# Convolution of a gated feed-forward layer: the accumulator of the three taps in PSUM instead of SBUF

## Chip, core and metric

The kernel runs on one core of a Trainium2 chip. The metric is the device time of one execution in microseconds (us); the median of three runs of the kernel before is 1090.98 us (1090.66 to 1093.48). A profile is one further execution, recorded by the hardware profiler: the one shown here took 1091.43 us, and the span of its recorded work is 1089.6 us.

The engines are named as the profile names them: PE multiplies matrices and writes its products to PSUM, PEld is the loading of its weights, DVE is the vector engine, ACT the scalar engine, POOL the GpSimd engine, and SP's queue issues the DMA transfers.

## What is computed

One layer of a diffusion backbone works on 512 latent tokens and 128 prompt tokens with the same weights, everything in 32-bit floats. Attention and a pooling mixer come first; the change is in the feed-forward part that follows. For a token matrix h (640 x 1024) it is

```
a, up = split(h @ w_ffn_in)                      # 1024 -> 2816 and 2816
a  = a[t-1] * w[0] + a[t] * w[1] + a[t+1] * w[2] + b     # along the tokens, per channel
x  = x + gate2 * ((silu(a) * up) @ w_ffn_out)
```

The convolution `dwconv3` runs over the 512 latent tokens and over the 128 prompt tokens as two separate sequences, with zeros beyond their ends. A final RMSNorm follows.

## The kernel before

**Tiles.** The 2816 channels are 22 tiles of 128 channels, which lie on the 128 partitions; the 640 tokens lie along the free dimension. Every 32-bit matrix product is made of three products of rounded halves (the high part of the weight with the high and the low part of h, and its low part with the high part of h). The 22 tiles form three groups of 8, 7 and 7 (`GROUPS`); after each group `out2_steps` multiplies the finished tiles with their rows of `w_ffn_out` and adds the result to x.

**One tile.** The two token halves (320 each) of `a` and `up` are not made by eight block products but by seven (a Strassen-like scheme). `product(i, p)` (line 1068) is one of the seven, p = 1 to 7, each 12 matmuls of 128x320, in two PSUM banks of tile i, `PS[i][0]` (named pf`i`A) and `PS[i][1]` (pf`i`C), and a bank of its own for product 2 (pb, from `bank1`, line 108, a pool of two banks). Both pf banks come from a pool of six (`banks`, line 997). The steps that read the products are `copy1`, `copy5`, `copy6` (ACT, PSUM to SBUF) and `add2`, `add3`, `add7` (DVE, one operand in PSUM). They leave the 640 values of `a` in the SBUF tile `av`, and part of `up` in the SBUF tile `c`. Product 3 ends in pf`i`C and `add3` is the last to read it there. Product 7 ends in pf`i`A, `add7` reads it, and only then may product 4 add to the same bank.

**The weights** need work too: POOL builds sums of weight blocks (`sums`, line 1030, four additions of 128x512 for a tile, both inputs in SBUF), ACT rounds them (`hi`, 1041), DVE subtracts to get the low parts (`lo`, 1058; tiles wlo_f and ul). The raw weights come by DMA into a pool of three buffers.

**The convolution** of tile i is `conv(i)` (line 1117): ACT writes `av * w[1] + b` into the SBUF tile `cv` (one instruction, 128x640), then four DVE instructions SCALAR_TENSOR_TENSOR add the taps in place: for the latent tokens 511 values shifted by one each way, for the prompt tokens 127 each way. Each reads `av` and `cv` and writes `cv`. `silu(i)` (1126) is one ACT instruction over `cv` in place; `glu2` (1129) and `glu1` (1132) multiply the halves of `cv` with `up`; `ghi` and `glo` (1136, 1139) split the product for the second matrix multiplication.

**Order.** All these steps run in a written order: `Pin` (142) makes every engine keep the order in which the code calls it, so that in the profile they all stand under line 150, and groups are told apart by their tiles. `cycle(i, ...)` (1425) is the order of one tile: it makes products 1, 2, 5, 6 and 3 of tile i and products 7 and 4 of tile j = i - 1, and in between the convolution of tile j and the weights of tile n = i + 1. On DVE the order of a cycle is: `add3(j)`, the four taps of tile j, `add2(i)`, `add7(j)`, `lo(n, 1)`, `glu2(j)`, `lo(n, 2)`, `lo(n, 3)`, then `glu1(j)`, which waits for product 4 of tile j, and `lo(n, 4)`. On PE it is products 1 and 2 of i, 7 of j, 5, 6 and 3 of i, 4 of j. Tiles 0 and 1 (`DIRECT`) are made directly and stand in another written order, `start` (1482); tile 2 is the first of the cycles' kind.

Of the kernel before, what the change touches and what calls it, by code (L numbers as in the profile page):

```python
# [13 lines left out]
AF = mybir.ActivationFunctionType  # L14
ALU = mybir.AluOpType
# [6 lines left out]
LAT = 512  # L22
PRO = 128
TOK = LAT + PRO
# [12 lines left out]
V_C, V_CC, V_N1, V_N2, V_PS, V_CW, V_CB, V_SUB, V_END = 0, 8, 16, 24, 32, 36, 102, 124, 125  # L37
# [30 lines left out]
def trunk_kernel(ctx: ExitStack, tc: tile.TileContext, a: dict, o: list):  # L68
# [39 lines left out]
    def bank1(name):  # L108
        return psB.tile([P, 512], F32, tag="B", name=name)
# [43 lines left out]
    dve, act, pool = Pin(nc.vector), Pin(nc.scalar), Pin(nc.gpsimd)  # L153
# [45 lines left out]
    vcol = const.tile([P, V_END], F32, tag="vcol", name="vcol")  # L199
# [820 lines left out]
    DIRECT = 2  # L1020
    R, S, W2, PS, PB, PD, AV, C22, CVS, GT = {}, {}, {}, {}, {}, {}, {}, {}, {}, {}
# [93 lines left out]
        dve.tensor_tensor(AV[i][:, HALF:], AV[i][:, HALF:], PS[i][1][:, :HALF], ALU.add)  # L1115

    def conv(i):
        av = AV.pop(i)
        cv = CVS[i] = pools["ffn"].tile([P, TOK], F32, tag="cv", name=f"cv{i}", bufs=3)
        w = [vcol[:, V_CW + j * NF + i:V_CW + j * NF + i + 1] for j in range(3)]  # L1120
        act.activation(cv, av, AF.Identity, bias=vcol[:, V_CB + i:V_CB + i + 1], scale=w[1])
        for s0, s1 in ((0, LAT), (LAT, TOK)):
            dve.scalar_tensor_tensor(cv[:, s0 + 1:s1], av[:, s0:s1 - 1], w[0], cv[:, s0 + 1:s1], ALU.mult, ALU.add)
            dve.scalar_tensor_tensor(cv[:, s0:s1 - 1], av[:, s0 + 1:s1], w[2], cv[:, s0:s1 - 1], ALU.mult, ALU.add)

    def silu(i):
        act.activation(CVS[i], CVS[i], AF.Silu)

    def glu2(i):
        dve.tensor_tensor(CVS[i][:, HALF:], CVS[i][:, HALF:], C22.pop(i), ALU.mult)  # L1130
# [294 lines left out]
    def cycle(i, first, end, after):  # L1425
# [17 lines left out]
        elif j is not None and j > first and first != DIRECT:  # L1443
            glo(j - 1)
        do(j, conv)
        do(n, sums, 0)
        add2(i)
# [5 lines left out]
        do(n, hi, 1)  # L1453
        do(n, lo, 1)
        do(j, silu)
        do(j, glu2)
        do(n, hi, 2)
# [24 lines left out]
    def start():  # L1482

        sums(2, 0)
        load(3, 0)
        conv(0)
        product(0, "G", "H")
        hilo(2, 2)
        sums(2, 1)
        load(3, 1)  # L1490
        product(1, "E", "F")
        copy6(1)
        silu(0)
        hi(2, 3)
        glu_direct(0)
# [10 lines left out]
        product(2, 5)  # L1506
        copy5(2)
        conv(1)
        hi(3, 2)
        lo(2, 4)  # L1510
        lo(3, 2)
        silu(1)
        sums(3, 1)
        product(2, 6)
# [68 lines left out]
```

## Time and profile before

| | |
|---|---|
| median of three runs | 1090.98 us (1090.66 to 1093.48) |
| profiled execution | 1091.43 us, span 1089.6 us |
| PE busy | 1038.0 us, 95% of the span |
| DVE busy | 851.6 us, 78% |
| ACT busy | 543.5 us, 50% |
| POOL busy | 320.8 us, 29% |
| the cycles of the three groups | 654 to 743, 806 to 894, 945 to 1031 us |
| PE / DVE busy there | 82.2 / 79.3 of 89 us, 85.1 / 81.1 of 88 us, 83.4 / 81.2 of 86 us |

The feed-forward part takes the last 450 us of the span. In the three stretches of cycles both PE and DVE are busy nearly all the time. An engine's busy time is the time that its instructions take in the record, and that includes the time in which an instruction has begun but is held up. Where an engine stands idle before an instruction, the profile names the instruction that released it.

### The profile page before, as it was taken

Reading aid. Unit: us, or ns where it says so; the run is one execution under the profiler, and the core shown is the slowest. Engines: PE = TensorE matmul, PEld = TensorE weight load, DVE = VectorE, ACT = ScalarE, POOL = GpSimd, SP = SyncE. Lnnn points to the kernel's source line nnn. Section 1 sums busy time; section 2 is a strip of 40 time slices with the busy share of each in tenths; the row PEclk is TensorE's granted clock in tenths of the full one; section 3 lists DMA queues with packets and bytes.
Section 4 is the critical chain, followed back from the end, with each engine's and each line's share of the span. In section 5 each row is a group of like instructions: output and inputs, shape, how many; then the busy total and the mean of one; then the engine's idle time right before and its main releaser. Section 6 shows DMA issues by size and latency. Waiting matters only on the chain.

```text
span 1089.6 us, 16713 instructions
## 1 busy us (share of the span) xinstructions
PE 1038.0 (95%) x6559; PEld 967.0 (89%) x6559; DVE 851.6 (78%) x1193; ACT 543.5 (50%) x906; POOL 320.8 (29%) x256
## 2 busy tenths in 40 slices
PE   6979999999999999999999999899989999999997
PEld 4778899999999999999998899898779998899986
DVE  5978978988887577776773579998889984699947
ACT  8646666666765552222242465554345542255524
POOL 4544224323222630000000005443374420444202
PEclk9999999999999999999999999999999999999999
DMA  9831212202112135545554022223442322323312
GB/s 312 247 88 51 62 32 69 59 25 71 38 43 59 41 96 157 165 140 159 154 190 141 1 78 59 83 92 93 127 128 82 94 68 68 97 78 94 119 38 97
DMA packets 128481, 106.10 MB, mean 97 GB/s; under 512 B 4174, under 2 KB 110206, under 8 KB 128403
## 3 DMA queue, kind: packets, MB, share of 16 engines
q1 hardware_dynamic: 126450, 101.93, 30.8%
q0 software_dynamic: 1232, 1.80, 0.8%
q8 instruction: 51, 0.84, 0.3%
q10 hardware_dynamic: 720, 1.31, 0.3%
q14 instruction: 28, 0.22, 0.1%
HBM read 101.36 MB, written 3.67 MB: 96 GB/s over the span
## 4 chain that ended last, share of the span: by engine, by line
PE 54%; DVE 28%; ACT 8%; issue 7%; POOL 1%; DMA 1%; SPq 0%; ACTq 0%; DVEq 0%; POOLq 0%
PE ps_g L157 10%; DVE cv L150 7%; PE psyb L157 5%; PE psk L157 3%; PE psu L157 3%; PE psya L157 3%; DVE wlo_f L150 3%; PE s L157 2%; PE acc L157 2%; PE po L157 2%; DVE nm L688 2%; PE psv L157 2%; PE psq L157 2%; ACT cv L150 1%; PE pat L160 1%
## 5 line engine op out<-in xcount | busy, mean ns | idle before, releaser
L150 POOL TENSOR_TENSOR s<-raw_fu 128x512 f32<-128x512 f32 x20 | 33.3, 1666 | 309.1 <-DVE spare L150 155.7
L150 DVE SCALAR_TENSOR_TENSOR cv<-av,vcol,cv 128x511 f32<-128x511 f32 (+1 forms) x80 | 88.8, 1130 | 12.1 <-ACT cv L150 10.8
L157 PE MATMUL ps_g<-hT,whi_g 128*128 128x320 f32 x512 | 96.7, 311 | 0.0
L157 PEld LDWEIGHTS ps_g<-hT,whi_g 128*128 128x128 f32 x512 | 80.2, 188 | 2.0 <-issue 1.5
L690 ACT ACTIVATE p<-s,nm 128x640 f32<-128x640 f32 (+1 forms) x80 | 56.7, 709 | 40.0 <-DVE nm L688 39.4
L688 DVE TENSOR_REDUCE nm<-s 128x1 f32<-128x640 f32 (+1 forms) x80 | 56.5, 709 | 12.4 <-PE s L157 11.0
L157 PE MATMUL psv<-whi_v,hT 128*128 128x256 f32 x320 | 66.0, 286 | 0.0
L157 PE MATMUL ps_g<-hT,wlo_g 128*128 128x320 f32 x256 | 58.3, 309 | 0.0
L150 DVE TENSOR_TENSOR wlo_f<-s,whi_f 128x1024 fp32r<-128x1024 f32 x40 | 51.0, 1298 | 4.7 <-ACT whi_f L150 4.6
L157 PE MATMUL s<-ks,qd 128*128 128x320 f32 x144 | 44.2, 318 | 10.7 <-DVE ks L599 7.1
L157 PEld LDWEIGHTS psv<-whi_v,hT 128*128 128x128 f32 x320 | 53.2, 192 | 0.3 <-ACT whi_v L126 0.3
L157 PE MATMUL psyb<-on,whi_pb 128*128 128x320 f32 x256 | 48.0, 309 | 0.0
L150 ACT CAST whi_f<-s 128x1024 fp32r<-128x1024 f32 x40 | 41.8, 1044 | 12.0 <-POOL s L150 11.9
L157 PE MATMUL psv<-wlo_v,hT 128*128 128x256 f32 x160 | 45.5, 284 | 0.9 <-DVE wlo_v L127 0.9
L157 PE MATMUL s<-ks,ql 128*128 128x320 f32 x144 | 42.9, 308 | 0.0
L157 PEld LDWEIGHTS ps_g<-hT,wlo_g 128*128 128x128 f32 x256 | 42.8, 188 | 0.0
L157 PE MATMUL psk<-hT,whi_k 128*128 128x320 f32 x224 | 42.6, 312 | 0.0
L157 PEld LDWEIGHTS psyb<-on,whi_pb 128*128 128x128 f32 x256 | 40.3, 188 | 0.5
L697 ACT ACTIVATE p<-p,z 128x640 f32<-128x640 f32 (+1 forms) x40 | 29.7, 744 | 20.0 <-DVE z L696 19.8
L157 PEld LDWEIGHTS s<-ks,qd 128*128 128x128 f32 x144 | 27.6, 192 | 13.4 <-POOL ry_q L562 6.8
L698 DVE SCALAR_TENSOR_TENSOR p<-p,z,p 128x640 f32<-128x640 f32 (+1 forms) x40 | 35.0, 878 | 5.4 <-ACT p L697 5.1
L150 POOL TENSOR_TENSOR acc_g<-acc_g,part_g 128x512 f32<-128x512 f32 x16 | 27.9, 1743 | 37.7 <-ACT part_g L150 36.8
(985 smaller groups left out, 3409.9 us busy)
## 6 DMA issues: line engine op xcount, KB each, us to landing
raw_fa<-in_w_ffn_in_dram SPq DMA_DIRECT2D x22, 512.0 KB, 3.8
raw_fu<-in_w_ffn_in_dram SPq DMA_DIRECT2D x22, 512.0 KB, 3.8
raw_fo<-in_w_ffn_out_dram SPq DMA_DIRECT2D x20, 512.0 KB, 3.6
raw_g<-in_w_in_dram SPq DMA_DIRECT2D x16, 512.0 KB, 4.9
raw_g<-in_w_ada_dram SPq DMA_DIRECT2D x16, 512.0 KB, 3.7
araw_sh<-in_w_ada_dram SPq DMA_DIRECT2D x8, 512.0 KB, 7.6
araw_sc<-in_w_ada_dram SPq DMA_DIRECT2D x8, 512.0 KB, 8.3
raw_v<-in_w_in_dram SPq DMA_DIRECT2D x8, 512.0 KB, 6.3
```

Of the source, the lines that this page charges most:

```text
L150: pin(getattr(self.eng, op)(*args, **kw))
L157: pin(nc.tensor.matmul(out, s, m, start=start, stop=stop, skip_group_check=more))
L160: pin(nc.tensor.transpose(out, x, ident))
L688: nc.vector.tensor_reduce(nm[:, i:i + 1], s, AX.XY, ALU.max, negate=True)
L690: nc.scalar.activation(p.rearrange("p (b n) -> p b n", b=s.shape[1]), s, AF.Exp, bias=nm[:, i:i + 1], accum_out=z[:, i:i + 1])
L697: nc.scalar.activation(p, p, AF.Copy, scale=z[:, 1:2])
L698: nc.vector.scalar_tensor_tensor(A[h, t], A[h, t], z[:, 0:1], p, ALU.mult, ALU.add)
```

## The change

For tiles 2 to 21 the running sum of the convolution is kept in PSUM: the 512 latent tokens in the bank pf`i`C, which `add3` was the last to read, and the 128 prompt tokens in a further bank `cvp` from the pool of two that product 2 uses. ACT's first step becomes two instructions (128x512 and 128x128), one for each bank. The four DVE instructions read `av` in SBUF and the sum in PSUM and write the sum in PSUM. `silu` becomes two instructions that read PSUM and write the SBUF tile `cv`, as the later steps expect it. Tiles 0 and 1 are unchanged.

```diff
     def conv(i):
         av = AV.pop(i)
         cv = CVS[i] = pools["ffn"].tile([P, TOK], F32, tag="cv", name=f"cv{i}", bufs=3)
         w = [vcol[:, V_CW + j * NF + i:V_CW + j * NF + i + 1] for j in range(3)]
-        act.activation(cv, av, AF.Identity, bias=vcol[:, V_CB + i:V_CB + i + 1], scale=w[1])
-        for s0, s1 in ((0, LAT), (LAT, TOK)):
-            dve.scalar_tensor_tensor(cv[:, s0 + 1:s1], av[:, s0:s1 - 1], w[0], cv[:, s0 + 1:s1], ALU.mult, ALU.add)
-            dve.scalar_tensor_tensor(cv[:, s0:s1 - 1], av[:, s0 + 1:s1], w[2], cv[:, s0:s1 - 1], ALU.mult, ALU.add)
+        if i < DIRECT:
+            SUMS[i] = cv[:, :LAT], cv[:, LAT:]
+        else:
+            SUMS[i] = PS[i][1], bank1(f"cvp{i}")[:, :PRO]
+        segs = tuple(zip(SUMS[i], (av[:, :LAT], av[:, LAT:])))
+        for c, x in segs if i >= DIRECT else ((cv, av),):
+            act.activation(c, x, AF.Identity, bias=vcol[:, V_CB + i:V_CB + i + 1], scale=w[1])
+        for c, x in segs:
+            dve.scalar_tensor_tensor(c[:, 1:], x[:, :-1], w[0], c[:, 1:], ALU.mult, ALU.add)
+            dve.scalar_tensor_tensor(c[:, :-1], x[:, 1:], w[2], c[:, :-1], ALU.mult, ALU.add)
+
+    SUMS = {}
 
     def silu(i):
-        act.activation(CVS[i], CVS[i], AF.Silu)
+        lat, pro = SUMS.pop(i)
+        cv = CVS[i]
+        for c, x in ((cv[:, :LAT], lat), (cv[:, LAT:], pro)) if i >= DIRECT else ((cv, cv),):
+            act.activation(c, x, AF.Silu)
```

On ACT, around the convolution of tile 16 (in the cycle of tile 17), the rows before are these; vcol holds the taps and the bias, whi_f and s belong to the weights of tile 18:

```order
L150 COPY av_9667<-pf17A 128x320
L150 ACTIVATE cv_9670<-av_9536,vcol 128x640
L150 COPY c_17_9693<-pf17C 128x320
L150 CAST whi_f_18_9695<-raw_fa_9588 128x1024
L150 ACTIVATE cv_9670<-cv_9670 128x640
L150 CAST whi_f_18_9701<-s_18_9676 128x1024
```

and in the changed kernel, at the same place:

```order
L150 COPY av_9709<-pf17A 128x320
L150 ACTIVATE pf16C<-av_9575,vcol 128x512
L150 ACTIVATE cvp_9713<-av_9575,vcol 128x128
L150 COPY c_17_9737<-pf17C 128x320
L150 CAST whi_f_18_9739<-raw_fa_9630 128x1024
L150 ACTIVATE cv_9712<-pf16C 128x512
L150 ACTIVATE cv_9712<-cvp_9713 128x128
L150 CAST whi_f_18_9746<-s_18_9720 128x1024
```

Each of the two ACT steps of the tile has become two instructions at its old place; nothing else on ACT moved.

On DVE the rows of the same cycle are, before (pb is product 2 of tile 17, pf16A holds product 7 of tile 16):

```order
L150 TENSOR_TENSOR av_9536<-av_9536,pf16C 128x320
L150 TENSOR_TENSOR g_9396<-cv_9538,g_9395 128x640
L150 SCALAR_TENSOR_TENSOR cv_9670<-av_9536,vcol,cv_9670 128x511 x2
L150 SCALAR_TENSOR_TENSOR cv_9670<-av_9536,vcol,cv_9670 128x127 x2
L150 TENSOR_TENSOR av_9667<-av_9667,pb_9641 128x320
L150 TENSOR_TENSOR c_16_9561<-c_16_9561,pf16A 128x320
L150 TENSOR_TENSOR wlo_f_18_9696<-raw_fa_9588,whi_f_18_9695 128x1024
L150 TENSOR_TENSOR cv_9670<-cv_9670,c_16_9561 128x320
```

and in the changed kernel:

```order
L150 TENSOR_TENSOR av_9575<-av_9575,pf16C 128x320
L150 TENSOR_TENSOR g_9435<-cv_9577,g_9434 128x640
L150 SCALAR_TENSOR_TENSOR pf16C<-av_9575,vcol,pf16C 128x511 x2
L150 SCALAR_TENSOR_TENSOR cvp_9713<-av_9575,vcol,cvp_9713 128x127 x2
L150 TENSOR_TENSOR av_9709<-av_9709,pb_9683 128x320
L150 TENSOR_TENSOR c_16_9602<-c_16_9602,pf16A 128x320
L150 TENSOR_TENSOR wlo_f_18_9740<-raw_fa_9630,whi_f_18_9739 128x1024
L150 TENSOR_TENSOR cv_9712<-cv_9712,c_16_9602 128x320
```

DVE's instructions keep number, shape and order; the four taps have another place for their sum. On PE, POOL and SP the order is the same in both kernels. PE has one wait more: product 2 of tile 4 lies in the bank that `cvp` of tile 2 had, and waits for the ACT instruction that reads it. From then on `cvp` and product 2 keep to one bank each of the two.

## Rows read from the trace of the kernel before

**Rows 1.** The page's part 4: the chain that ended last, by engine.
```profile
PE 54%; DVE 28%; ACT 8%; issue 7%; POOL 1%; DMA 1%; SPq 0%; ACTq 0%; DVEq 0%; POOLq 0%
```

**Rows 2.** Two cycles: stretch, its length, busy us (instructions) by engine, granted clock, DMA.
```profile
846.00:858.27 12.27, 12.27 (x87) 12.27 (x85) 11.94 (x15) 6.39 (x10) 5.85 (x4) 1.00 0.29 85
980.29:993.05 12.76, 12.48 (x86) 12.22 (x85) 12.43 (x15) 6.72 (x11) 6.39 (x4) 1.00 0.29 83
```

**Rows 3.** Weight loading's waits, 684 to 1035: total us, times, longest.
```profile
PEld pf2A L157 <- DVE c L150: 3.2, 1, 3.2
...
PEld pf8A L157 <- DVE c L150: 2.0, 1, 2.0
PEld pf15A L157 <- DVE c L150: 1.7, 1, 1.7
PEld pf3A L157 <- DVE c L150: 1.5, 1, 1.5
...
PEld pf19A L157 <- DVE c L150: 0.8, 1, 0.8
PEld pf4A L157 <- DVE c L150: 0.8, 1, 0.8
...
PEld pf5A L157 <- DVE c L150: 0.6, 1, 0.6
PEld pf17A L157 <- DVE c L150: 0.5, 1, 0.5
PEld pf16A L157 <- DVE c L150: 0.5, 1, 0.5
PEld pf12A L157 <- DVE c L150: 0.4, 1, 0.4
PEld pf18A L157 <- DVE c L150: 0.2, 1, 0.2
```

**Rows 4.** DVE's timeline, 680 to 690 us: start, duration, instruction, [idle before <- releaser].
```profile
681.67 5.07 DVE L150 SCALAR_TENSOR_TENSOR cv<-av,vcol,cv 128x511 f32<-128x511 f32 x4 [0.64 <-ACT cv L150]
...
687.06 0.47 DVE L150 TENSOR_TENSOR c<-c,pf2A 128x320 f32<-128x320 f32 x1
...
689.28 1.21 DVE L150 TENSOR_TENSOR wlo_f<-s,whi_f 128x1024 fp32r<-128x1024 f32 x1
```

**Rows 5.** PE's timeline, 684 to 690 us, the last matmul before the wait.
```profile
684.34 0.31 PE L157 MATMUL pf3C<-mg,wlo_f 128*128 128x320 f32 x1
```

**Rows 6.** DVE's timeline, 964 to 990 us: the taps of tile 16.
```profile
971.82 5.77 DVE L150 SCALAR_TENSOR_TENSOR cv<-av,vcol,cv 128x511 f32<-128x511 f32 x4 [0.26 <-ACT cv L150]
```

**Rows 7.** POOL's timeline, 938 to 995 us: one of four additions beside them.
```profile
972.80 1.63 POOL L150 TENSOR_TENSOR s<-s,raw_fa 128x512 f32<-128x512 f32 x1
```

**Rows 8.** DVE's timeline, 878 to 900 us: the taps of tile 13, POOL idle.
```profile
885.73 2.18 DVE L150 SCALAR_TENSOR_TENSOR cv<-av,vcol,cv 128x511 f32<-128x511 f32 x4 [0.26 <-ACT cv L150]
```

**Rows 9.** DVE's timeline, 373 to 403 us: the same operation with pr, pm in PSUM.
```profile
382.48 1.01 DVE L899 SCALAR_TENSOR_TENSOR on<-oraw,sub,pr 128x320 f32<-128x320 f32 x2 [1.51 <-PE pr L157]
...
386.34 1.01 DVE L921 SCALAR_TENSOR_TENSOR mix<-pm,vcol,mix 128x320 fp32r<-128x320 f32 x2 [0.48 <-ACT mix L920]
```

**Rows 10.** POOL's timeline, 373 to 403 us: what ran beside the second of them.
```profile
385.96 1.58 POOL L902 TENSOR_TENSOR on<-on,on 128x640 fp32r<-128x640 f32 x1 [3.88 <-PE pm L157]
```

**Rows 11.** Instructions on tile cv: duration ns min/median/max, first and last start, forms.
```profile
L150 DVE SCALAR_TENSOR_TENSOR cv<-av,vcol,cv x80: 340/1273/1684, 681.7 to 1035.5; 128x511 f32<-128x511 f32 x40, 128x127 f32<-128x127 f32 x40
L150 ACT ACTIVATE cv<-cv x22: 737/738/744, 663.3 to 1035.9; 128x640 f32<-128x640 f32 x22
...
L150 ACT ACTIVATE cv<-av,vcol x20: 919/924/926, 680.7 to 1032.2; 128x640 f32<-128x640 f32 x20
```

**Rows 12.** Instructions of line 433, ACT with scale and bias, columns as above.
```profile
L433 ACT ACTIVATE hT<-xT,sh,sc x16: 477/642/818, 24.1 to 55.4; 128x512 fp32r<-128x512 f32 x8, 128x128 fp32r<-128x128 f32 x8
```

**Rows 13.** The stretch 829.36 to 832.77 us, columns as in Rows 2.
```profile
829.36:832.77 3.41, 3.41 (x15) 3.41 (x14) 3.41 (x6) 2.03 (x4) 0.00 (x0) 0.50 0.51 149
```

**Rows 14.** DVE's timeline, 796 to 846 us: a low part of weights while POOL adds.
```profile
811.44 2.32 DVE L150 TENSOR_TENSOR wlo_f<-s,whi_f 128x1024 fp32r<-128x1024 f32 x1
```

## Prediction, made before the changed kernel ran

> **What bounds the kernel now.** I read the chain of waits first: PE holds 54% of it and DVE 28% [rows 1], so the question is where DVE holds PE up. The windows by cycle answer it for the feed-forward part. A cycle has 84 matmuls. Where PE never waits, it takes 12.27 us, 0.146 us a matmul; elsewhere it takes 12.76 us and DVE is busy for 12.43 of them [rows 2]. So the cycles run at the pace of DVE, and PE's own pace lies 0.49 us lower. The waits of the weight loads name the place: eleven times PE stands before product 4 of a tile (pf2A to pf19A) until DVE has done `add7` (c) [rows 3]. In DVE's order the four taps of the convolution stand just ahead of `add2` and `add7`, so their length is what PE waits for.
>
> The timeline of DVE shows why they are long. Beside POOL's four additions the four taps of tile 16 take 5.77 us; with POOL idle those of tile 13 take 2.18 us [rows 6 to 8]. One tap takes from 0.34 us (127 values, alone) to 1.68 us [rows 11]; from the 2.18 us a 511-wide one alone is 2.18 / 2 - 0.34 = 0.75 us. Both inputs of each tap are in SBUF, and so are those of POOL's additions.
>
> **The taps with their sum in PSUM.** The trace has the same operation with one input in PSUM: two of 320 values take 1.01 us with POOL idle and 1.01 us while POOL runs a 1.58 us subtraction with both inputs in SBUF [rows 9, 10]. So one input in PSUM takes POOL's hold off DVE. I price a tile's four taps at 2.18 us, against 5.77: 3.6 us less on DVE for each of the 14 or so tiles whose convolution meets POOL's additions; the last two of each group do not (tile 13 is one).
>
> What the trace does not show is a DVE instruction that writes PSUM, or reads and writes one bank. Its ends: below, rows 9 give 1.01 us for two of 320, and nothing there makes PSUM dearer, so 2.18 us or some tenths under it; above, 5.77 us, the length under POOL. I take 2.18, the value of the row that is nearest in operation.
>
> [...] A straight line from 0.34 us at 127 values to 0.75 at 511 gives 0.55 at 320, 1.09 for two, and the row with PSUM has 1.01 [rows 8, 9, 11]: no surcharge is seen. [...]
>
> **ACT.** One instruction of 0.92 us becomes one of 512 values and one of 128; with scale and bias such rows lie between 0.48 and 0.82 us [rows 11, 12], so 1.30 us at most in sum, 0.38 more. DVE needs only the first to start, 0.82 us, so it starts 0.1 us earlier. SiLU goes from 0.74 us to two instructions; from PSUM I have no row of it, and bound it by 0.74 for each piece, so 0.74 us more at the most; with the two fixed parts I take 0.1 to 0.2. ACT is busy for 6.7 of 12.76 us in a cycle [rows 2], and with 0.4 to 1.1 us more it still has 4.5 us free: nothing on the path. Without that cover it would be 20 x 0.5 = 10 us.
>
> **Banks.** pf`i`C is next written by product 5 of a tile three cycles later, so holding it until `silu` costs nothing. Product 2 of tile 4 now waits for the SiLU of tile 2. That follows the taps and is due by 683.75 + 1.5 = 685.3 (times as worked out below); the product starts two products, 24 matmuls, behind PE's restart, at 684.6 + 3.5 = 688.1. After that `cvp` and product 2 use different banks. 0 us, and if the cover went, one wait once.
>
> **The sum.** The eleven waits: 3.2 + 2.0 + 1.7 + 1.5 + 0.8 + 0.8 + 0.6 + 0.5 + 0.5 + 0.4 + 0.2 = 12.2 us [rows 3]. What is late next decides how much of it comes back.
>
> - First wait (tile 2): the taps start 0.1 us earlier than 681.67, at 681.57, and end at 683.75. `add7` ended 0.79 us behind the taps (687.53 against 686.74) [rows 4], so now at 684.54. PE itself is ready 0.146 us after its last matmul began, at 684.49 [rows 5]. Left: 0.05 us and the way of the signal, 0.1 us of 3.2.
> - The other ten: the taps give 3.6 us back, each wait is 2.0 us or less. Nothing is left.
> - Then PE sets the pace: DVE's cycle is 12.76 - 0.26 (idle) - 5.77 + 2.18 = 8.9 us [rows 2, 6, 8] against PE's 12.27.
>
> [...] I take it that without the wait the fall goes too, with 60%.
>
> Sum: -(12.2 - 0.1) - 1.2 = -13.3 us, or -12.1 with the fall kept. The waits that DVE or ACT causes elsewhere (start of the groups, the gate between group 1 and 2) are not touched: POOL's part in them is the same. From the profiled 1091.43 us this gives 1078.1. The median of the runs is 0.45 us lower than the profiled execution, so **1077.7 us**.
>
> **Rivals.**
>
> - *PSUM taps cost more.* A tap that reads and writes one bank might run at half speed: 4.4 us a tile. Then the first wait keeps 2.2 us more, the others still vanish (DVE's cycle is 8.9 + 2.2 = 11.1, under 12.27): 1079.9. Only with taps of 12.27 - (8.9 - 2.18) = 5.55 us or more is the pace DVE's again: 1091, no change. For it: no row shows a DVE write to PSUM. Against: the reads of rows 9 show nothing extra. The end at 1091: 8%.
> - *Another wait takes over.* PE would stand before product 5, 6 or 1 because the rounded weights (POOL, then ACT, then DVE) come late. For it: in a cycle DVE's last low parts follow POOL's last addition. Against: DVE has 3.4 us of slack in a cycle, `lo(n, 1)`, which frees the buffer for the next DMA, moves forward with `add7`, and POOL too loses its rival. If half of the waits come back so: 1091.0 - 6.7 = 1084.3. 13%.
> - *The collision only moves* (the slower side). POOL's four additions per cycle, 6.4 us together [rows 2, 7], need to read SBUF as before; where they do not meet the taps, they can meet the low parts, `glu2` and `glo`. A low part that met one took 2.32 us instead of 1.21 [rows 4, 14], 1.1 us more. With all four additions meeting one each, DVE's cycle is 8.9 + 4.4 = 13.3 us, 0.54 over 12.76, and for 17 cycles that is 9 us: 1100. It decides from 3.5 collisions a cycle on; up to three (12.2 us) cost nothing, and PE sets the pace. Against it: the additions run in one piece beside the taps today, and of that stretch the taps, `add2` and `add7` (all with PSUM now) cover 3 us. So I expect one or two hits. 4%.
>
> The price of a hit is the row's 1.1 us. [...]
>
> **Chances and range.** Forecast 75% (with the fall of the clock kept in two cases of five: 1078.9), another wait 13%, no gain 8%, slower 4%. About 0.3%, 3.3 us, is what the measurement can tell. Faster: 75 and 13, less a little for gains under 3.3 us: 0.86. Within: 0.09. Slower: 0.05. The range: below, a DVE that is early might also shorten waits at the groups' starts and in the gate, of up to 3 us: 1074.7. Above, to half of the gain, 1084.5. The forecast's own range is 1076 to 1080.5.
>
> **What will show it.** Right: the taps (named pf`i`C and cvp) at 0.7 to 0.8 and 0.34 us whether POOL runs or not; DVE's busy time down by some 40 us; no wait of PE for c over 0.3 us; cycles of 12.3 us; POOL's additions shorter or the same. ACT's busy time up by 8 to 15 us. Wrong step by step: taps that stretch with POOL (the price in PSUM), low parts of 1.8 to 2.3 us in most cycles (the moved collision), PE's waits on wlo_f or whi_f in the cycles (another wait), a granted clock of 0.50 in a new place. The forecast is wrong if the cycles keep 12.7 us, or if they fall to 12.3 us and the stretches between the groups grow by as much.

## Result, and the profile after

The changed kernel takes 1081.12 us (median of 6 runs, 1078.91 to 1083.97), the kernel before 1093.37 us (6 runs, 1090.66 to 1095.63): a ratio of 0.9891, 95% interval 0.9868 to 0.9914, or 12.3 us less. 1077.7 us were predicted, with a range of 1074.7 to 1084.5. A control, the changed kernel once more on another occasion, gave 1079.51 us and a ratio of 0.9882 (0.9866 to 0.9899). The profiled execution took 1082.84 us, its span is 1081.1 us.

Read the chain first, the answer to [rows 1]: DVE's share fell from 28% to 19%, PE's rose from 54% to 66%. Part 1 of the page stands below it; before, DVE was busy for 851.6 us, ACT for 543.5 us and POOL for 320.8 us.

```profile
PE 66%; DVE 19%; ACT 6%; issue 4%; DMA 2%; POOL 1%; SPq 1%; ACTq 0%; DVEq 0%; POOLq 0%
...
PE 1038.2 (96%) x6559; PEld 970.1 (90%) x6559; DVE 822.4 (76%) x1193; ACT 549.5 (51%) x946; POOL 317.5 (29%) x256
```

Three windows: two cycles, to be held against [rows 2], and the matmuls that follow product 4 of tile 8, where the granted clock had fallen to 0.50 before [rows 13]. Columns: stretch, length, busy us (instructions) of PE, PEld, DVE, ACT and POOL, granted clock, DMA share, GB/s.

```profile
858.00:870.26 12.26, 12.26 (x86) 12.26 (x85) 10.12 (x15) 7.08 (x12) 5.63 (x5) 1.00 0.27 86
971.43:983.69 12.26, 12.26 (x86) 12.26 (x85) 10.04 (x17) 6.98 (x13) 5.81 (x4) 1.00 0.30 86
...
825.65:829.17 3.52, 3.52 (x26) 3.52 (x25) 3.52 (x3) 1.57 (x3) 1.14 (x1) 1.00 0.31 88
```

The cycle that took 12.76 us now takes 12.26, PE never stands in it, and DVE has 2.2 us to spare in the second of the two. The waits of the weight loads from 670 to 1035 us (total us, times, longest) answer to [rows 3]:

```profile
PEld pb_g L157 <- DVE bl_g L250: 2.7, 2, 1.9
PEld pf2A L157 <- ACT av L150: 1.6, 1, 1.6
...
PEld pf5A L157 <- ACT av L150: 1.3, 1, 1.3
PEld pf8C L157 <- DVE wlo_f L150: 0.8, 1, 0.8
PEld pf9A L157 <- DVE wlo_f L150: 0.8, 1, 0.8
PEld pf3A L157 <- ACT av L150: 0.6, 1, 0.6
PEld pf4A L157 <- DVE c L150: 0.2, 1, 0.2
PEld pf2A L157 <- DVE c L150: 0.2, 1, 0.2
```

Of eleven waits for c, 12.2 us, two of 0.2 us are left. One is new: 1.3 us at tile 5. The timelines of DVE and POOL at the taps of tile 17, against [rows 6, 7] (start, duration, instruction):

```profile
976.80 1.55 DVE L150 SCALAR_TENSOR_TENSOR pf17C<-av,vcol,pf17C 128x511 f32<-128x511 f32 x2
978.25 0.74 DVE L150 SCALAR_TENSOR_TENSOR cvp<-av,vcol,cvp 128x127 f32<-128x127 f32 x2
```

```profile
975.88 1.95 POOL L150 TENSOR_TENSOR s<-raw_fu 128x512 f32<-128x512 f32 x1 [5.09 <-DMA raw_fu<-in_w_ffn_in_dram]
977.91 1.29 POOL L150 TENSOR_TENSOR s<-s,raw_fa 128x512 f32<-128x512 f32 x1
```

From 976.80 to 978.99 the four taps take 2.19 us, with POOL adding beside them all but 0.08 us of the time, where they took 5.77; POOL's second addition takes 1.29 us where it took 1.63. Its first began beside DVE's subtraction for g, with both inputs in SBUF, ahead of the taps.

**What the profiled execution hides.** Its first matmul of the feed-forward part (on pf0A) starts at 638.1 us; before it was 633.6. From there to the end of the span are 443.0 us against 456.0: 13.0 us less, but 4.5 us are lost ahead of the change, where both programs are the same. Two windows of the first 100 us show it, in the kernel before, the changed kernel, and the control (columns as above):

```profile
40.00:60.00 20.00, 18.67 (x131) 16.18 (x129) 18.66 (x26) 11.53 (x18) 14.28 (x12) 1.00 0.69 163
...
80.00:100.00 20.00, 16.80 (x113) 16.56 (x114) 16.30 (x23) 10.60 (x22) 8.30 (x6) 0.87 0.12 37
```

```profile
40.00:60.00 20.00, 18.66 (x113) 15.63 (x112) 17.93 (x26) 12.69 (x20) 12.42 (x12) 0.83 0.65 152
...
80.00:100.00 20.00, 12.68 (x77) 12.44 (x78) 16.21 (x22) 10.84 (x20) 8.21 (x7) 0.83 0.04 11
```

```profile
40.00:60.00 20.00, 18.68 (x120) 16.19 (x118) 18.67 (x26) 11.51 (x18) 14.25 (x12) 0.91 0.69 162
...
80.00:100.00 20.00, 15.71 (x100) 15.48 (x101) 16.23 (x25) 10.72 (x21) 8.70 (x6) 0.83 0.06 14
```

Look at the granted clock, third from the right. Where a mean is under 1.00, a part of the window ran at 0.50: taken by single microseconds, the first 100 us show 0.50 from 78.4 to 85.3 us in the kernel before, from 32.5 to 35.9, 53.0 to 59.8 and 83.7 to 90.5 us in the changed kernel, and 1.00 elsewhere. That is nothing of 40 to 60 us before, 0.17 x 2 x 20 = 6.8 us of it in the changed kernel, and PE began 113 matmuls there instead of 131. The control reached pf0A at 635.2 us. From 100 us to pf0A none of the three profiles shows a clock under 1.00. So for all kernels below the time from pf0A to the end of the span, "the feed-forward part", stands beside the time of the runs.

### The profile page after: what moved, and what is told of

It is laid out like the page before. It is cut to its first block, busy times and chain, and to the rows that moved or that the text cites. A ratio compares the mean times of both kernels' runs of the same rounds, so it can differ in the third digit from the quotient of the medians.

```text
span 1081.1 us, 16773 instructions
## 1 busy us (share of the span) xinstructions
PE 1038.2 (96%) x6559; PEld 970.1 (90%) x6559; DVE 822.4 (76%) x1193; ACT 549.5 (51%) x946; POOL 317.5 (29%) x256
## 4 chain that ended last, share of the span: by engine, by line
PE 66%; DVE 19%; ACT 6%; issue 4%; DMA 2%; POOL 1%; SPq 1%; ACTq 0%; DVEq 0%; POOLq 0%
PE ps_g L157 10%; PE psyb L157 5%; PE psk L157 3%; PE psu L157 3%; PE psya L157 3%; PE pb L157 3%; PE s L157 2%; PE po L157 2%; PE psq L157 2%; DVE nm L688 2%; PE psv L157 2%; PE acc L157 1%; PE pat L160 1%; DVE ks L599 1%; DVE p L698 1%
## 5 line engine op out<-in xcount | busy, mean ns | idle before, releaser
L150 POOL TENSOR_TENSOR s<-raw_fu 128x512 f32<-128x512 f32 x20 | 30.1, 1504 | 299.4 <-DVE spare L150 155.8
L688 DVE TENSOR_REDUCE nm<-s 128x1 f32<-128x640 f32 (+1 forms) x80 | 56.5, 709 | 12.4 <-PE s L157 11.0
L157 PEld LDWEIGHTS psv<-whi_v,hT 128*128 128x128 f32 x320 | 53.5, 193 | 0.3 <-ACT whi_v L126 0.3
L150 DVE TENSOR_TENSOR wlo_f<-raw_fa,whi_f 128x1024 fp32r<-128x1024 f32 x22 | 34.5, 1567 | 21.8 <-ACT whi_f L150 21.6
L157 PE MATMUL pb<-mg,whi_f 128*128 128x320 f32 x176 | 38.9, 307 | 0.0
```

Source lines behind the costliest of these rows:

```text
L150: pin(getattr(self.eng, op)(*args, **kw))
L157: pin(nc.tensor.matmul(out, s, m, start=start, stop=stop, skip_group_check=more))
L688: nc.vector.tensor_reduce(nm[:, i:i + 1], s, AX.XY, ALU.max, negate=True)
```

## The experiments

| kernel | us, median | ratio to before (95%) | feed-forward part |
|---|---|---|---|
| before | 1091 to 1094 | 1 | 456.0 |
| changed; control | 1081.12; 1079.51 | 0.9891 (0.9868 to 0.9914); 0.9882 (0.9866 to 0.9899) | 443.0; 443.2 |
| e1: SBUF, no additions | 1072.44 | 0.9810 (0.9788 to 0.9833) | 436.9 |
| e2: PSUM, no additions | 1074.03 | 0.9815 (0.9789 to 0.9842) | 436.2 |
| e3: ACT's split alone | 1091.81 | 0.9990 (0.9974 to 1.0005) | 454.7 |
| e4: first tap reads SBUF | 1084.80 | 0.9913 (0.9889 to 0.9936) | 446.9 |
| e5: 4 taps more | 1084.83 | 0.9923 (0.9898 to 0.9948) | 447.8 |
| e6: 8 taps more | 1105.76 | 1.0129 (1.0093 to 1.0165) | 467.8 |
| e7: latent sum alone | 1081.07 | 0.9889 (0.9864 to 0.9913) | 444.3 |
| e8: prompt sum alone | 1084.66 | 0.9915 (0.9884 to 0.9946) | 446.4 |
| e9: prompt of tiles 0, 1 too | 1078.04 | 0.9865 (0.9848 to 0.9883) | 442.3 |
| e10: order on ACT | 1080.65 | 0.9886 (0.9868 to 0.9904) | 442.2 |
| e11: e9 and e10 | 1078.12 | 0.9874 (0.9857 to 0.9891) | 442.6 |

### e1 and e2: without POOL's additions

The same edit in the kernel before (e1) and in the changed one (e2):

```diff
     def sums(i, b, dst=None):
-        ra, ru = R[i, 0], R[i, 1]
...
-            pool.tensor_tensor(s[:, :4, :], ra[:, 4:, :], S[i, 0][:, 4:, :], ALU.subtract)
-            pool.tensor_tensor(s[:, 4:, :], ra[:, :4, :], ru[:, :4, :], ALU.subtract)
+        S[i, b] = R[i, b]
```

> The sum stays in SBUF as before the change; POOL's four additions per tile are left out (the products that took sums and differences of weights take the raw weights). Theory (DVE's taps and POOL's additions, all with two inputs in SBUF, hold each other up): the four taps take 2.2 us in every tile from 2 on, the eleven waits for c (12.2 us) go without any PSUM, 1078 to 1081 us; up to 2 us less if stretched low parts at the groups' starts go too. Rival (PSUM as such is the quicker place, or summing in place in SBUF is slow): taps stay at 5 us and more, 1090 to 1094 us.

> The changed kernel with POOL's additions left out in the same way. Theory: taps 2.2 us as in the changed kernel, time within 3 us of the SBUF kernel without additions and 0 to 3 us under the changed kernel (waits for weights at the groups' starts and at tile 5). Rival (PSUM has a worth of its own beside the collision): 8 us or more under the SBUF kernel without additions. Second rival (the collision has moved to the low parts and still costs PE time in the cycles): 4 us or more under the changed kernel, cycles shorter than 12.26 us.

The taps of e1 (sum in SBUF; duration ns min/median/max):

```profile
L150 DVE SCALAR_TENSOR_TENSOR cv<-av,vcol,cv x80: 344/548/755, 678.0 to 1016.5; 128x511 f32<-128x511 f32 x40, 128x127 f32<-128x127 f32 x40
```

Without additions no tap in SBUF is longer than 0.755 us, where the maximum was 1.684 [rows 11]; the waits for c are gone without any PSUM. So it is the collision with the additions, and no worth of PSUM as such is seen: the two differ by 0.7 us in the feed-forward part and their intervals overlap almost wholly. That bears out the theory of both, and refutes e1's rival and e2's first.

The size I gave both was wrong: they end 7 to 9 us under the changed kernel (6 to 7 in the feed-forward part), not 0 to 3. What is left of e2's waits from 684 to 1035 us shows where, and the window is one of its cycles:

```profile
PEld pb_g L157 <- DVE bl_g L250: 1.7, 2, 0.9
PEld acc010A L157 <- DVE wlo_fo L150: 1.2, 2, 0.9
```

```profile
951.38:963.65 12.27, 12.27 (x87) 12.27 (x86) 9.10 (x15) 7.10 (x12) 0.00 (x0) 1.00 0.30 87
```

The waits at tiles 2, 3, 5, 8 and 9 are gone: 1.6 + 0.6 + 1.3 + 0.8 + 0.8 + 0.4 for c = 5.5 us, and 1.0 us of pb_g, of the 6.8 us between 443.0 and 436.2. So e2's second rival was right in its size (4 us and more under the changed kernel) and falls by its place, since the cycles are 12.27 us in e2 too: the additions still cost PE time, but at the groups' starts and before pb_g, the gate between groups 1 and 2. How much of that is the collision, and how much that the weights wait for POOL at all, these two runs do not separate. The window also measures DVE's cycle with no addition in its way: 9.10 us.

### e3: ACT's split alone

```diff
-            SUMS[i] = PS[i][1], bank1(f"cvp{i}")[:, :PRO]
+            SUMS[i] = cv[:, :LAT], cv[:, LAT:]
```

> Only ACT's part of the change: its two steps split into 512 and 128 values as in the changed kernel, the sum in SBUF. Theory: taps 5 to 5.8 us beside POOL, the waits stay, 1090 to 1094 us. Rival (ACT's shorter first piece, or a SiLU that starts earlier, gives the gain): taps may be long but PE waits under 6 us in all, 1085 us or less.

DVE's timeline at tile 17, and two of PE's waits:

```profile
983.00 5.89 DVE L150 SCALAR_TENSOR_TENSOR cv<-av,vcol,cv 128x511 f32<-128x511 f32 x4
```

```profile
PEld pf2A L157 <- DVE c L150: 3.2, 1, 3.2
...
PEld pf8A L157 <- DVE c L150: 1.8, 1, 1.8
```

The taps are as before, the waits for c come to 11.0 us where they were 12.2, and the interval holds 1. The feed-forward part is 1.3 us shorter, so the two pieces of ACT are at most a tenth of the gain.

### e4: a tap with two inputs in SBUF and its output in PSUM

ACT writes the start value into cv too, and the first tap of each pair reads it there:

```diff
-        for c, x in segs:
-            dve.scalar_tensor_tensor(c[:, 1:], x[:, :-1], w[0], c[:, 1:], ALU.mult, ALU.add)
+        if i >= DIRECT:
+            act.activation(cv, av, AF.Identity, bias=vcol[:, V_CB + i:V_CB + i + 1], scale=w[1])
+        for (c, x), d in zip(segs, (cv[:, :LAT], cv[:, LAT:])):
+            dve.scalar_tensor_tensor(c[:, 1:], x[:, :-1], w[0], d[:, 1:], ALU.mult, ALU.add)
```

(c is the sum in PSUM, d the same values in cv.)

> The changed kernel, but the first tap of each pair reads the sum from SBUF (ACT writes the start value there too, 0.92 us more on ACT per tile) and writes PSUM; the second reads and writes PSUM. Theory (it is the second SBUF input that collides): first taps of 511 beside POOL 1.65 to 1.8 us, second ones 0.75 us; 3.1 to 4.2 us a tile; DVE still under PE's 12.26 us a cycle in most, 1080 to 1085 us. Rival (an output in PSUM is enough): first taps 0.75 us as well, 1079 to 1082 us.

DVE's timeline at tile 17, and the addition of POOL that ran beside the last three of these taps:

```profile
977.24 1.73 DVE L150 SCALAR_TENSOR_TENSOR pf17C<-av,vcol,cv 128x511 f32<-128x511 f32 x1 [1.35 <-ACT cv L150]
979.01 0.76 DVE L150 SCALAR_TENSOR_TENSOR pf17C<-av,vcol,pf17C 128x511 f32<-128x511 f32 x1
979.67 0.61 DVE L150 SCALAR_TENSOR_TENSOR cvp<-av,vcol,cv 128x127 f32<-128x127 f32 x1
```

```profile
978.50 1.62 POOL L150 TENSOR_TENSOR s<-raw_fa,s 128x512 f32<-128x512 f32 x1
```

Of two taps with the same size and output, the one with both inputs in SBUF takes 1.73 us, the next 0.76. In eight tiles the first long tap takes 1.72 to 1.74 us; no second one exceeds 0.756. The inputs decide, not the output; the rival is refuted. The short tap took 0.61 us rather than 1.3. The addition beside it ended at 980.12, 0.45 us after the tap began; a tap that loses only the rest of a running addition would fit this, but no run tests it. In most cycles DVE still has room, and PE's waits for c grow only at tiles 2 and 4 (1.9 and 1.6 us).

### e5 and e6: how much room DVE has

```diff
+        for c, x in segs * 1 if i >= DIRECT else ():
+            dve.scalar_tensor_tensor(c[:, 1:], x[:, :-1], 0.0, c[:, 1:], ALU.mult, ALU.add)
+            dve.scalar_tensor_tensor(c[:, :-1], x[:, 1:], 0.0, c[:, :-1], ALU.mult, ALU.add)
```

(e6: segs * 2.)

> The changed kernel with four more taps of weight 0 per tile on the same sum in PSUM: 2.2 us more on DVE for each of 20 tiles, 44 us in all. Theory (PE sets the pace now, DVE has 2 us or more to spare in a cycle): the cycles stay at 12.3 us; only the tiles whose add7 came last (2 and 4, 0.2 us each now) wait 2 us more: 1081 to 1087 us. Rival (DVE still sets the pace, because the stretched low parts took the room): 2.2 us more in each of some 17 cycles, 1110 us or more.

> The same with eight more taps, 4.4 us more on DVE per tile. Two estimates for a DVE-bound cycle: 10.05 us busy now and 4.4 make 14.5 us, 2.2 us over PE's 12.26 in each of 17 cycles, 1118 us, if POOL's additions go on stretching DVE's low parts; 8.9 + 4.4 = 13.3 us, 1.0 us over, 1098 us, if the longer taps in PSUM cover the additions and no low part is stretched any more. Rival (there is slack of 4 us and more): under 1087 us.

A cycle of e5, then one of e6, with DVE's and POOL's timelines in e6:

```profile
963.56:975.82 12.26, 12.26 (x86) 12.26 (x85) 11.99 (x21) 6.99 (x12) 5.82 (x4) 1.00 0.32 91
```

```profile
973.21:985.97 12.76, 12.49 (x87) 12.23 (x85) 12.43 (x23) 7.13 (x12) 5.72 (x4) 1.00 0.28 83
```

```profile
992.20 1.42 DVE L150 SCALAR_TENSOR_TENSOR pf17C<-av,pf17C 128x511 f32<-128x511 f32 x2
...
995.90 0.48 DVE L150 TENSOR_TENSOR av<-av,pb 128x320 f32<-128x320 f32 x1
...
996.70 1.22 DVE L150 TENSOR_TENSOR wlo_f<-raw_fa,whi_f 128x1024 fp32r<-128x1024 f32 x1
...
998.24 2.35 DVE L150 TENSOR_TENSOR wlo_f<-s,whi_f 128x1024 fp32r<-128x1024 f32 x2
```

```profile
989.23 1.91 POOL L150 TENSOR_TENSOR s<-raw_fu 128x512 f32<-128x512 f32 x1 [6.83 <-DMA raw_fu<-in_w_ffn_in_dram]
...
993.85 1.29 POOL L150 TENSOR_TENSOR s<-raw_fa,raw_fu 128x512 f32<-128x512 f32 x1
```

With e5's four taps more the cycles stay at 12.26 us: DVE does not set the pace. The feed-forward part is 4.8 us longer: tile 2's wait for c grew to 2.0 us (expected; at tile 4 none came), the granted clock was 0.50 for 3.41 us behind it, and the waits before pb_g grew from 2.7 to 4.7 us (neither expected).

In e6 three of the four additions lie beside taps that read PSUM, the first one in its second half, and the three low parts take 1.22 + 2.35 us, their unhindered length. DVE is busy for 12.43 us, as before the change, and the cycle is as long as then. The eight zero taps, from 992.20 to 995.90, take 3.7 us, not 4.4. Without them DVE is busy for 8.7 us in e6's cycle; in e2's, without additions, it is 9.1. That bears out the prediction's 8.9 us for DVE's unhindered cycle. The 1105.76 us of e6 lie between its two estimates. Some 8 of the 25 us by which its feed-forward part is longer are the cycles; the rest stands at the groups' ends and starts (4.6 us for c at tile 20, 3.9 at tile 2, 1.8 each at 8 and 15) and in three stretches at 0.50 of the clock, 13.7 us in all, where the changed kernel has none from pf0A to 1077 us.

### e7 and e8: one of the two sums

```diff
-            SUMS[i] = PS[i][1], bank1(f"cvp{i}")[:, :PRO]
+            SUMS[i] = PS[i][1], cv[:, LAT:]
```

(e8: cv[:, :LAT] and the bank cvp.)

> Only the latent sum (512 values) in PSUM, the prompt sum (128) in SBUF. Theory (a tap's length beside POOL is set by whom it collides with, not by its size; what counts is that DVE's cycle falls below PE's): long taps 0.75 us, short ones 1.3 to 1.4 us beside POOL, 4.2 us a tile; most of the gain, 1081 to 1087 us. Rival (the gain is shared by size: 80% of the values): short taps about 0.4 us, 1081 us.

> Only the prompt sum (128 values) in PSUM, the latent sum in SBUF. Theory: long taps 1.6 to 1.7 us beside POOL, short ones 0.35 us, 4.0 us a tile, DVE's cycle about 12 us: most of the gain although only a fifth of the values lie in PSUM, 1081 to 1087 us. Rival (the gain goes with the values): a fifth of 12 us, 1089 to 1092 us.

DVE's timelines at the taps, e7 (tile 18) and then e8 (tile 17):

```profile
984.97 1.53 DVE L150 SCALAR_TENSOR_TENSOR pf18C<-av,vcol,pf18C 128x511 f32<-128x511 f32 x2
986.41 2.60 DVE L150 SCALAR_TENSOR_TENSOR cv<-av,vcol,cv 128x127 f32<-128x127 f32 x2
```

```profile
980.29 3.26 DVE L150 SCALAR_TENSOR_TENSOR cv<-av,vcol,cv 128x511 f32<-128x511 f32 x2 [0.16 <-ACT cv L150]
983.47 0.73 DVE L150 SCALAR_TENSOR_TENSOR cvp<-av,vcol,cvp 128x127 f32<-128x127 f32 x2
```

Two taps of 127 values cost 2.60 us in SBUF beside POOL, two of 511 cost 3.26: over the 0.35 and 0.755 us of e1 and the changed kernel that is a loss of 0.95 us for a short tap and 0.87 for a long one. The collision is paid per instruction, hardly per value. Either sum alone takes 1.6 to 1.9 us off DVE's 5.77 a tile; DVE's cycle had to lose 0.49 us to come down to PE's pace, so each brings most of the gain of 13.0 us in the feed-forward part: four fifths of the values in PSUM (e7) 11.7 us, one fifth (e8) 9.6. For e8 the time refutes the rival (1089 us and more); e7's time is the 1081 us of its rival too, and there only the length of the short taps, 1.3 us and not 0.4, refutes it.

### e9 to e12: the start, and a control

e9 gives tiles 0 and 1 a bank cvp for their prompt sum; e10 moves steps on ACT; e11 does both.

```diff
-        if i < DIRECT:
-            SUMS[i] = cv[:, :LAT], cv[:, LAT:]
-        else:
-            SUMS[i] = PS[i][1], bank1(f"cvp{i}")[:, :PRO]
+        SUMS[i] = cv[:, :LAT] if i < DIRECT else PS[i][1], bank1(f"cvp{i}")[:, :PRO]
...
-        silu(1)
         sums(3, 1)
         product(2, 6)
         copy6(2)
+        silu(1)
...
-        ghi(0)
-        ghi(1)
...
         do(j, conv)
+        if i == DIRECT + 1:
+            ghi(0)
+            ghi(1)
```

> The changed kernel with the prompt sum of tiles 0 and 1 in PSUM as well (a bank cvp each). One short tap of 1.38 us beside POOL in each becomes 0.35 us: 1.0 us less on DVE ahead of PE's waits of 1.35 us at 681 us and 0.3 us at 685 us. Theory (DVE with its stretched taps sets the start of the feed-forward part): 0.5 to 1.5 us less from the first product on. Rival (ACT's order or the DMA sets it): no change.

> The changed kernel with two steps moved on ACT: the copy of product 6 of tile 2 ahead of the SiLU of tile 1, which waits for taps until 680.0 us, and the two gate casts of tiles 0 and 1 behind the convolution of tile 2. Theory: the wait of 1.35 us (av, tile 2) and of 0.3 us (av, tile 3) go; up to half of it comes back as a wait for c at tile 2, whose add7 ends 0.2 us late already: 0.5 to 1.5 us less. Rival: DVE is the bound behind it, all of it comes back at tile 2 or at tile 5 (where weights come late): no change.

> Both edits together: the waits at 681 and 685 us go and c of tile 2 comes 1 to 1.5 us sooner. Theory: 1.5 to 2.5 us less than the changed kernel from the first product on. Rival (tile 5's weights, behind DVE and POOL, take it back): under 0.5 us less.

> The changed kernel itself, run beside the three. If the 4.5 us that its profiled execution took longer up to the feed-forward part come from where the granted clock fell in the first 100 us, and not from the change, then its profile may show either of two times at the first product of the feed-forward part, 633.5 or 638 us, and from there on 442 to 444 us; a cost of the change would keep it at 638 us.

The three lie 0.6 to 1.0 us under the control in the feed-forward part, one profile each, and their intervals overlap with its: no version is shown to beat the changed kernel. e10's waits say why: those at 681 and 685 us and at tile 5, 3.5 us, are gone, and one of 2.2 us stands in their place, with the granted clock at 0.50 for 3.41 us behind it. ACT's queue shows where it comes from: ACT first waits for DVE, and the gate casts now stand ahead of its copy of product 5:

```profile
PEld pf3C L157 <- ACT c L150: 2.2, 1, 2.2
```

```profile
681.36 0.78 ACT L150 ACTIVATE pf2C<-av,vcol 128x512 f32<-128x512 f32 x1 [1.76 <-DVE av L150]
...
682.47 1.33 ACT L150 CAST g<-cv 128x640 fp32r<-128x640 f32 x2
683.71 0.41 ACT L150 COPY c<-pf3C 128x320 f32<-128x320 f32 x1
```

In e9 the waits for av keep 1.2 us at tile 2, 1.0 at tile 3 and 1.2 at tile 5, so 1 us less on DVE did not shorten them. The control answers its question: 635.2 us to pf0A, neither 633.5 nor 638. Kernels with taps in PSUM reached it between 633.4 (e4) and 638.2 us (e8). So the 4.5 us are not a cost of the change, but there are not just two times either: in these profiles the time goes by the number of stretches at 0.50 (see the last section), and what sets that number is open.

## Why the prediction was right

- **The taps.** Priced at 2.18 us a tile, they take 2.19, beside POOL or not, and with that the waits that they caused went: the mechanism held. The bound above (5.77) and rival 1 fell. No surcharge for an input in PSUM is seen: a long tap takes 0.756 us at most in PSUM, 0.755 in SBUF without additions (e1).
- **The eleven waits.** 12.2 us were to go but for 0.1; 0.4 are left. The cycle is 12.26 us, 12.27 were forecast. DVE's unhindered cycle, forecast at 8.9 us, is 8.7 to 9.1 (e6, e2).
- **The clock.** The forecast's 1.2 us are the stretch of [rows 13], where the clock was 0.50: 15 matmuls began in its 3.41 us, and at 0.146 us each 23.4 would have, 8.4 x 0.146 = 1.2. In the changed kernel 26 began in 3.52 us there, at 1.00. The fall behind tile 8 is gone, held for 60% likely. That its wait brought it is not shown: e3 kept a wait of 1.8 us at tile 8 and had no fall there, but one behind its 3.2 us at tile 2, where the kernel before, with the same wait, had none; e5 and e10 had one behind a wait of 2.0 and 2.2 us, e7 none behind 2.1. So 1.2 us of the sum are in part luck.
- **DVE's busy time: the step that was mis-sized.** 40 us less were forecast, 29.2 came. The taps of the two traces, tiles 0 and 1 included, fell from 99.7 to 53.5 us, 46.2 less; but the low parts wlo_f took some 5.7 us more, `glu2` 6.6 and the two other low parts `ul` and g 4.5. So rival 3 was right in its mechanism and wrong in its end: the collision did move. Instructions on cv (`glu2`) and the low parts of weights, before and after the change:

```profile
L150 DVE TENSOR_TENSOR cv<-cv,c x20: 476/478/494, 688.9 to 1036.7; 128x320 f32<-128x320 f32 x20
L150 DVE TENSOR_TENSOR wlo_f<-raw_fa,whi_f x22: 1210/1215/2199, 628.7 to 1016.5; 128x1024 fp32r<-128x1024 f32 x22
```

```profile
L150 DVE TENSOR_TENSOR cv<-cv,c x20: 478/486/1596, 690.3 to 1027.7; 128x320 f32<-128x320 f32 x20
```

```profile
L150 DVE TENSOR_TENSOR wlo_f<-raw_fa,whi_f x22: 1219/1362/2334, 633.2 to 1006.3; 128x1024 fp32r<-128x1024 f32 x22
```

- It moved into DVE's room and cost PE nothing in the cycles: DVE's 10.0 to 10.1 us in the two windows above are 1 us over the 9.1 without additions, one hit of 1.1 us, where more than two are needed to pass PE's 12.27 (9.1 + 3 x 1.1 = 12.4). The prediction expected one or two. Six of the 20 `glu2` took 1.57 to 1.60 us instead of 0.48, a loss of 1.1 us for an instruction of 0.48 as for a low part of 1.21 (2.33 at most, in the row above). So short ones lose as much, and the prediction's price of 1.1 us a hit, read from a low part, holds for `glu2` too.
- **Rival 2 in small.** The wait of 1.3 us at tile 5, with POOL, DVE and ACT in this order: POOL's last addition, itself stretched, ends late, 69.3 us after pf0A where it was 68.0, while PE gets there sooner without its waits for c. DVE's low part waits for the weights and stands ahead of the multiplication of cv, ACT's cast of g waits for that, and behind it stands the copy av that PE waits for.

```profile
705.14 2.26 POOL L150 TENSOR_TENSOR s<-raw_fa,raw_fu 128x512 f32<-128x512 f32 x1
```

```profile
708.52 1.23 DVE L150 TENSOR_TENSOR wlo_f<-s,whi_f 128x1024 fp32r<-128x1024 f32 x1 [2.26 <-ACT whi_f L150]
709.66 0.48 DVE L150 TENSOR_TENSOR cv<-cv,pf3A 128x320 f32<-128x320 f32 x1
```

```profile
707.44 1.05 ACT L150 CAST whi_f<-s 128x1024 fp32r<-128x1024 f32 x1 [2.35 <-POOL s L150]
...
710.23 0.72 ACT L150 CAST g<-cv 128x640 fp32r<-128x640 f32 x1 [1.22 <-DVE cv L150]
710.86 0.42 ACT L150 COPY av<-pf5A 128x320 f32<-128x320 f32 x1
```

- **ACT.** 0.79 + 0.45 us for the 0.92 of the first step, 0.60 + 0.28 for the SiLU's 0.74: 0.32 and 0.14 us more, inside the bounds. Its busy time rose by 6.0 us, under the 8 to 15 forecast. Twenty tiles of this make 9.2, but busy time counts an overlap once, and in the record the second piece begins 0.07 us before the first ends. No wait for a bank appeared.
- **The sum.** -13.3 us were forecast, the feed-forward part shows -13.0. Its terms are 11.8 us of waits for c and 1.2 of the clock; two that were not forecast nearly cancel, by luck: 1.3 us more at tile 5, 1.1 less before pb_g. The time missed by 3.4 us (the control by 1.8). Of these, 2.4 lie in the start: the forecast took 1090.98 us for the kernel before, and its six runs gave 1093.37; 1.0 is the difference, 12.3 against 13.3. The part ahead of the change, taken to be equal in both, varied by 4.8 us over the profiles.

## What to carry to other kernels

Where DVE's instructions with two inputs in SBUF are stretched beside POOL's, and DVE is on the path, giving each of them one input from PSUM took it out of the collision here (four taps 2.19 us beside POOL instead of 5.77); the output's place did not matter (e4: 1.73 and 0.76 us with the same output in PSUM; [rows 9, 10]: 1.01 us for two, with POOL or without, for an output in SBUF). Count instructions, not values: a tap of 127 values lost 0.95 us, one of 511 0.87 (e7, e8). And look where the engine's cycle falls under that of the next bound: either half of this change brought three quarters to nine tenths of the gain (e7, e8), and the hits that the additions then dealt elsewhere cost nothing in the cycles (12.26 us, 12.27 without additions, e2). Outside them the additions still cost 6 to 7 us (e1, e2).

## What the runs showed of the hardware

- With both inputs in SBUF and beside POOL's additions, a tap of 127 values took about 1.3 us and one of 511 values 1.6 to 1.7, against 0.35 and 0.755 without additions (e7, e8, e1).
- POOL loses too, in places: in the changed kernel an addition took 1.29 us beside taps that read PSUM (at 977.91), and 2.26 beside a low part that reads SBUF (at 705.14); one at 969.49 took 1.30 beside a low part that itself took 2.33.
- Two taps of 511 values with the constant 0.0 as their weight took 1.42 us, two with a column of vcol 1.55 (e6, at 992.20 and 990.10).
- Up to 100 us the same instructions ran with one stretch at 0.50 of the clock in six profiles (6.8 us long in the kernel before), which reached pf0A at 633.4 to 633.9 us, with two in five (635.1 to 635.4) and with three in three (636.5 to 638.2; 3.4, 6.8 and 6.8 us long in the changed kernel). Kernels of both kinds, with taps in SBUF and in PSUM, are among the six.
